# A two-layer hybrid decoder on one core: the last four retention gates as a block product of seven, and a few pieces of work moved

## The chip, the cores and the metric

The kernel runs on one NeuronCore of a Trainium2 chip. It is written so that one program computes the whole decoder. TensorE (PE) multiplies, ScalarE (ACT) and VectorE (DVE) take its results out of PSUM and prepare operands in SBUF, GpSimd (POOL) issues a part of the transfers, and SyncE (SP) the rest. The metric is the time of one execution on the device in microseconds (us); of several runs the median is given. Everything is float32 at the boundary.

## The reference

Two layers on 512 tokens of width 1024. With `x` the stream, one layer is

```
h  = rmsnorm(x) ; z = h @ w_in
aq, ak, av, rq, rk, rv, rg, ga, gb = split(z)
A  = window_attention(rope(aq), rope(ak), av, sinks)          # 8 heads, window 128
B  = retention(rq, rk, rv)                                    # 4 heads, 256 values each
B  = B * rsqrt(mean(B*B per head) + eps) * silu(rg)
y  = sigmoid(ga) * (A @ w_a) + sigmoid(gb) * (B @ w_b)
x  = x + y @ w_out
x  = x + relu(rmsnorm(x) @ w_up)**2 @ w_down
```

and a last rmsnorm follows. The part `rg` is 1024 columns of `z`: eight chunks of 128, two for each retention head. `silu(rg)` gates the retention's normalised output.

## The kernel before, in words

**Products.** A number is held as a sum of two rounded halves, `hi` and `lo`, and each product is three matmuls: hi by hi, hi by lo, lo by hi (`products`, L390 to L392). Activations lie transposed: 128 features on the partitions, 512 tokens (`T`) along the columns, so that `xh[:, k, :]`, `xl[:, k, :]` are the halves of eight feature tiles `k`. The scale 1/rms of the tokens (`rstd`) is applied behind the products.

**Weights.** They come in units of 128x1024. `unit_order` lists them; `unit` hands out the next and has those up to three ahead (`SPLIT`) split: ScalarE rounds `hi` (L338), VectorE subtracts for `lo` (L339). Four buffers each hold `hi` and `lo`, five hold the raw unit. SP's queue loads them in that order.

**A chunk** (`chunk`) is 128 output columns for all tokens: 8 tiles `k` by 3 matmuls of 512 columns, one unit of weights.

**A block product of seven.** The value projection (`values`, for `rv`), the output projection (`output`, for `wo`) and the MLP's blocks are made from seven products of half size where the plain way needs eight. They need sums and differences of quarters of the weights and of the activations. For the weights, POOL's queue writes sums into DRAM with accumulating transfers (`sum_steps`), and VectorE adds two more (`add_values`, L318); the jobs of `sum_steps` are let go one by one by `pace`, which every second call copies one column on POOL and issues the next step behind it. For the activations, `Turned` loads `x` again, four tiles at a time into two buffers (`load`, L878), and makes the differences and their splits (`build`, L888 to L896): `turned[1]` to `turned[4]`. `build(0)` makes the first half of all of them, `build(2)` the second.

**Order.** The program is written in the order in which it should run, and a scheduler then orders the instructions of each engine; the order is fixed when the kernel is built, and each engine takes its instructions one after the other. `issue_after` binds what stands in it to come behind a given instruction. Attention and retention are generators (`background`) that are moved on a step at a time from within the chunks.

**A layer** runs so: queries, keys and values of the attention (`group`, then two chunks); eight chunks of `gate_a`, with the attention in between; `qk(0)`; gate chunks `rg` 0 to 3 (`put_rg`); the attention's end (`drain`), its last output `whole` split into `a_h` and `a_l`; `qk(1)` with `turned.build(0)`; gate chunks `rg` 4 and 5; the A projection (`w_a`, four units, result into `mixed` at L1142) with `turned.build(2)` behind its second unit; `values`; `qk(2)`, `qk(3)` with the retention of heads 0 and 1; gate chunks `rg` 6 and 7; four chunks of `gate_b`; half of the B projection (`w_b`, a `group`); the other four chunks of `gate_b`; the other half of `w_b`; `output`; the MLP.

A gate chunk's result is scaled (L988) and put through `silu` (L997, L998) where it stands. In `Head`, `outputs` copies the retention's output out of PSUM into a tile `rr` (L1044) and squares it for the norm (L1046); `finish` multiplies the gate with the inverse norm (L1066), then with `rr` (L1067), and splits the result into `ret`.

The **MLP** begins with `sum_input(0)` in the first up projection and `sum_input(2)` within the first down block (`down(0, ...)`), each making the differences of the MLP's input and their splits (L525 to L539). In the last layer `turn_x` transposes `x` (L1259) and writes it out for the final sums: the first half within `output`, the second, for four token blocks, in the first up projection. In layer 1 the first `group` multiplies all high halves first (`by_halves`, L405), and the ssq matmuls of `Rms.finish` (L608) spread the factors over the partitions.

Names with `r_` and a number, and `late`, are SBUF tiles of a pool of slots, used for whatever is split.

Of the kernel before, what the change touches and what calls it, by code (L numbers as in the profile page):

```python
# [17 lines left out]
P = 128  # L18
# [25 lines left out]
N_IN = 38  # L44
# [12 lines left out]
def unit_order(layer):  # L57

    order = [("w_in", i) for i in range(4 + 2 + 8 + 2 + 4 + 2 + 2)]
    order += [("w_a", i) for i in range(4)]  # L60
    order += [("rv", part, u) for part in range(7) for u in range(2)]
    order += [("w_in", i) for i in range(24, 34)]
    order += [("w_b", i) for i in range(4)]
    order += [("w_in", i) for i in range(34, 38)]
# [51 lines left out]
def decoder(ctx, tc, xT, x_first, w_in, w_rv, w_a, w_b, w_wo, w_up, w_pair, w_down, w_end, tables, decay, band, g_last, out):  # L116
# [63 lines left out]
    def load_until(n):  # L180
# [27 lines left out]
    MIXING = {"rv": w_rv, "wo": w_wo}  # L208
    sums_mix = {
        name: [dram.tile([2, P, 2 * UNIT], F32, name=f"sums_{name}{l}") for l in range(DEPTH)] for name in MIXING  # L210
    }

    def sum_steps(layer):
# [8 lines left out]
        for name, at in (("rv", 0), ("wo", 14)):  # L222
            jobs[at:at] = [(sums_mix[name][layer][u], MIXING[name][layer, u], 2 * UNIT) for u in range(2)]
# [90 lines left out]
    def add_values(i):  # L314
        part = order[i][2]
        if part in (2, 4):
            raws[i] = raws.pop(i - 2)
            nc.vector.tensor_tensor(raws[i], raws[i], raws.pop(i - 4), ALU.add)  # L318
# [75 lines left out]
    latest, behind = [None], []  # L394

    def by_halves(banks, weights, moving, ks, cols, meanwhile):

        hi, lo = weights
        for w, low in ((hi, 0), (lo, 0), (hi, 1)):
            if meanwhile and w is lo:  # L400
                meanwhile()
            for j, k in enumerate(ks):
                for c, ps in enumerate(banks):
                    first, final = k == 0 and w is hi and not low, k == KD - 1 and low
                    latest[0] = nc.tensor.matmul(ps, w[:, cols(j, c)], moving[k][low], start=first, stop=bool(final)).ins  # L405
# [177 lines left out]
    class Rms:  # L583
# [30 lines left out]
    def layer_body(layer):  # L614
# [366 lines left out]
        def put_rg(i):  # L981
            def put(ps):
# [6 lines left out]
                if i >= 4:  # L989
                    pace(rg[i])  # L990
                    silu(i)

            return put

# [13 lines left out]
        class Head:  # L1008
# [5 lines left out]
            def scores(self, js):  # L1014
# [14 lines left out]
                if js[-1] == NB - 1:  # L1029
                    slots.give(*rq.pop(h), *rk.pop(h))  # L1030
                    self.rr, self.sq = [], []

            def outputs(self, e):
# [7 lines left out]
                if e == 0:  # L1041
                    self.both = big("rr")
                r = self.both[:, e, :]
                nc.scalar.activation(r, ps, AF.Copy)  # L1044
                q = temp("sq")
                nc.scalar.activation(q, ps, AF.Square)  # L1046
                pace(r)
                self.rr.append(r)
# [29 lines left out]
        def retention(pair):  # L1078
# [23 lines left out]
            while 4 * pair + 3 not in rg:  # L1102
                yield
# [23 lines left out]
        for i in (4, 5):  # L1127
            chunk("w_in", layer, xs, put_rg(i))

# [19 lines left out]
        load_decay(0)  # L1149
        values(turned)  # L1150
# [5 lines left out]
        for i in (6, 7):  # L1156
            chunk("w_in", layer, xs, put_rg(i))
# [7 lines left out]
        for c in range(4):  # L1165
# [48 lines left out]
        TOKENS = (slice(0, H), slice(H, T))  # L1214
# [23 lines left out]
        for c in range(4, KD):  # L1238
# [18 lines left out]
        def turn_x(ps, b, i):  # L1257
# [10 lines left out]
            t = gain_tile[:, 2, :] if b == NB - 1 and i else temp("y")  # L1268
# [11 lines left out]
        def output():  # L1280
# [23 lines left out]

            def both(t):
                return t.rearrange("p (a t) -> p a t", t=H)
# [53 lines left out]
            ms.free(3, 4)  # L1360
            put(1, 0, b, -1)
# [30 lines left out]
        def sum_input(ks):  # L1392
# [9 lines left out]
            sums.rest(ks, b, (2, 3))  # L1402
# [328 lines left out]
        def first_hooks():  # L1731
            used = []

            def at0():
                used.append(column_factors())
                sum_input(0)

            def at1():
                if last:
                    used.append(bank(ps_aux, "xt"))  # L1740
                    for n in range(NB):
                        turn_x(used[n % 2], n, 1)

            return at0, at1

        for e in range(N_BLOCK):
# [15 lines left out]
            else:  # L1762
                down(e, into, None if e else lambda: sum_input(2))
# [42 lines left out]
def _w_in_units(w):  # L1806
# [20 lines left out]
    units += _units_chunks(w, O_RG + T + r(2 * P))  # L1827
    units += qk(2) + qk(3)
    units += _units_chunks(w, O_RG + T + 2 * P + r(2 * P))
# [12 lines left out]
def _mixing_blocks(w):  # L1842
# [8 lines left out]
    return blocks  # L1851

# [44 lines left out]
def _laid_out(x, g_mix, w_in, sinks, w_a, w_b, w_out, g_mlp, w_up, w_down, g_final):  # L1897
# [11 lines left out]
        "w_in": _stack(w_in, _w_in_units),  # L1909
        "w_rv": _stack(w_in, lambda w: _mixing_blocks(w[:, O_RV : O_RV + D])),  # L1910
# [30 lines left out]
```

## Time and profile before

| what | us |
|---|---|
| three runs | 1461.82, 1461.87, 1464.63 |
| the profiled execution | 1464.35 |
| its span, first to last instruction | 1462.3 |
| TensorE busy | 1450.0 |
| VectorE busy | 1169.0 |
| ScalarE busy | 969.0 |
| POOL busy | 222.3 |
| mean granted TensorE clock | 0.999 |

The profile's page and views give starts and durations in us from the span's start. "PE" is TensorE's multiplying, "PEld" its loading of weights, which overlaps. A matmul's end is modelled and includes its way through the array, so two that follow each other overlap in the list; how long a row of them takes is read from their starts. In a timeline row the last bracket is the idle time before it and what ended it. The chain of waits is followed back from the last instruction to what released each step.

### The profile page before, as it was taken

Reading aid. Unit: us, or ns where it says so; the run is one execution under the profiler, and the core shown is the slowest. Engines: PE = TensorE matmul, PEld = TensorE weight load, DVE = VectorE, ACT = ScalarE, POOL = GpSimd, SP = SyncE. Lnnn points to the kernel's source line nnn. Section 1 sums busy time; section 2 is a strip of 40 time slices with the busy share of each in tenths; the row PEclk is TensorE's granted clock in tenths of the full one; section 3 lists DMA queues with packets and bytes.
Section 4 is the critical chain, followed back from the end, with each engine's and each line's share of the span. In section 5 each row is a group of like instructions: output and inputs, shape, how many; then the busy total and the mean of one; then the engine's idle time right before and its main releaser. Section 6 shows DMA issues by size and latency. Waiting matters only on the chain.

```text
span 1462.3 us, 22150 instructions
## 1 busy us (share of the span) xinstructions
PE 1450.0 (99%) x8041; PEld 1265.4 (87%) x8041; DVE 1169.0 (80%) x1762; ACT 969.0 (66%) x1592; POOL 222.3 (15%) x329
## 2 busy tenths in 40 slices
PE   9999999999999999999999999999999999999998
PEld 7888888888988999999888888888889799999997
DVE  6978876876898888888778788687778988788885
ACT  6657556543687777777756575565437777777775
POOL 0011012112101111111201110112120111111120
PEclk9999999999999999999999999999999999999999
DMA  7598369899745777666955983797885477777664
GB/s 257 177 288 225 103 174 299 232 244 255 224 119 195 192 197 190 165 184 179 307 178 172 290 222 111 217 291 219 222 210 174 137 198 201 191 192 197 178 185 146
DMA packets 96428, 297.57 MB, mean 203 GB/s; under 512 B 11328, under 2 KB 11456, under 8 KB 90432
## 3 DMA queue, kind: packets, MB, share of 16 engines
q0 software_dynamic: 35936, 125.58, 37.2%
q1 hardware_dynamic: 59664, 169.27, 33.4%
q8 instruction: 63, 1.03, 0.3%
q10 hardware_dynamic: 720, 1.31, 0.2%
q14 instruction: 45, 0.37, 0.1%
HBM read 256.54 MB, written 115.87 MB: 255 GB/s over the span
## 4 chain that ended last, share of the span: by engine, by line
PE 96%; ACT 1%; DMA 1%; DVE 1%; issue 0%; DVEq 0%; ACTq 0%
PE mm L390 23%; PE mm L391 23%; PE mm L392 23%; PE wo L1296 5%; PE b L390 3%; PE b L391 3%; PE b L392 3%; PE rv L392 2%; PE rv L390 2%; PE rv L391 2%; PE mm L405 2%; PE score L773 1%; PE pT L738 1%; PE r L392 1%; PE r L391 1%; PE r L390 1%
## 5 line engine op out<-in xcount | busy, mean ns | idle before, releaser
L338 ACT ACTIVATE hi<-raw 128x1024 fp32r<-128x1024 f32 (+1 forms) x387 | 394.1, 1021 | 263.4 <-PE mm L391 146.9
L339 DVE TENSOR_TENSOR lo<-raw,hi 128x1024 fp32r<-128x1024 f32 (+1 forms) x388 | 452.7, 1174 | 107.4 <-ACT hi L338 105.3
L390 PE MATMUL mm<-xh,hi 128*128 128x512 f32 (+1 forms) x976 | 343.8, 356 | 1.8 <-ACT xh L413 1.0
L391 PE MATMUL mm<-xl,hi 128*128 128x512 f32 (+1 forms) x976 | 344.6, 356 | 0.0
L392 PE MATMUL mm<-xh,lo 128*128 128x512 f32 (+1 forms) x976 | 340.4, 355 | 0.0
L390 PEld LDWEIGHTS mm<-xh,hi 128*128 128x128 f32 x976 | 185.2, 190 | 27.7 <-ACT xh L413 1.7
L391 PEld LDWEIGHTS mm<-xl,hi 128*128 128x128 f32 x976 | 185.3, 190 | 24.2
L392 PEld LDWEIGHTS mm<-xh,lo 128*128 128x128 f32 x976 | 183.9, 190 | 23.6
L391 PE MATMUL mm<-r,hi 128*128 128x256 f32 (+1 forms) x608 | 189.2, 311 | 0.0
L392 PE MATMUL mm<-r,lo 128*128 128x256 f32 (+1 forms) x608 | 189.0, 311 | 0.0
L390 PE MATMUL mm<-r,hi 128*128 128x256 f32 (+1 forms) x608 | 186.6, 311 | 0.5 <-ACT mm L1471 0.5
L390 PEld LDWEIGHTS mm<-r,hi 128*128 128x128 f32 x608 | 115.8, 190 | 8.8 <-ACT mm L1471 0.7
L391 PEld LDWEIGHTS mm<-r,hi 128*128 128x128 f32 x608 | 115.8, 190 | 8.0
L392 PEld LDWEIGHTS mm<-r,lo 128*128 128x128 f32 x608 | 115.8, 190 | 6.3
L1619 POOL DMA_DIRECT2D y<-eu x56 | 62.4, 1354 | 374.4 <-DVE eu L1604 373.8
L391 PE MATMUL mm<-lo,r 128*128 128x512 f32 (+1 forms) x276 | 104.3, 387 | 0.0
L392 PE MATMUL mm<-hi,r 128*128 128x512 f32 (+1 forms) x276 | 101.3, 387 | 0.0
L390 PE MATMUL mm<-hi,r 128*128 128x512 f32 (+1 forms) x276 | 98.4, 390 | 0.9 <-ACT eu L1614 0.6
L390 PE MATMUL b<-hi,r 128*128 128x512 f32 x180 | 70.5, 392 | 1.6 <-DVE eu L1604 1.2
L391 PE MATMUL b<-lo,r 128*128 128x512 f32 x180 | 70.3, 390 | 0.0
L1296 PE MATMUL wo<-r,hi 128*128 128x256 f32 x384 | 69.4, 283 | 0.0
L392 PE MATMUL b<-hi,r 128*128 128x512 f32 x180 | 67.9, 390 | 0.0
(323 smaller groups left out, 2682.5 us busy)
## 6 DMA issues: line engine op xcount, KB each, us to landing
raw<-w_in_in SPq DMA_DIRECT2D x73, 512.0 KB, 5.8
sums_down<-w_down_in POOLq DMA_DIRECT2D x30, 1024.0 KB, 11.6
sums_up<-w_pair_in POOLq DMA_DIRECT2D x56, 512.0 KB, 10.9
raw<-w_down_in SPq DMA_DIRECT2D x45, 512.0 KB, 7.6
raw<-w_pair_in SPq DMA_DIRECT2D x84, 256.0 KB, 3.7
y<-y POOLq DMA_DIRECT2D x63, 256.0 KB, 9.4
y<-eu POOLq DMA_DIRECT2D x61, 256.0 KB, 8.1
raw<-sums_down SPq DMA_DIRECT2D x30, 512.0 KB, 7.4
```

The costliest lines, as they stand in the source:

```text
L338: state["high"] = nc.scalar.activation(hi[:, at], raw[:, at], AF.Copy).ins
L339: nc.vector.tensor_tensor(lo[:, at], raw[:, at], f32(hi[:, at]), ALU.subtract)
L390: nc.tensor.matmul(ps, ah, bh, start=start and i == 0, stop=False, **more)
L391: nc.tensor.matmul(ps, ah, bl, start=False, stop=False, **more)
L392: latest[0] = nc.tensor.matmul(ps, al, bh, start=False, stop=stop and i == n - 1, **more).ins
L405: latest[0] = nc.tensor.matmul(ps, w[:, cols(j, c)], moving[k][low], start=first, stop=bool(final)).ins
L738: nc.tensor.transpose(pt[:, i * P : (i + 1) * P], sm[:, at : at + P], ident)
L773: nc.tensor.matmul(ps[:, g * w : (g + 1) * w], q_s[g][:, c, at], part[:, keys], start=i == 0, stop=i == 1)
L1296: latest[0] = nc.tensor.matmul(o, w[:, cols], v, start=start and first and n % 2 == 0 and w is hi and v is vh, stop=final and w is lo, ski ...
L1619: nc.gpsimd.dma_start(y[:, 2 * j + m, i * T : (i + 1) * T], t, **how)
```

## The change

The last four gate chunks of each layer leave the unit order and become a block product of seven over 512 features, 256 columns and the two halves of the tokens. Its function, `last_gates`, runs between the A projection and `values`:

```diff
-    order = [("w_in", i) for i in range(4 + 2 + 8 + 2 + 4 + 2 + 2)]
+    order = [("w_in", i) for i in range(4 + 2 + 8 + 2 + 4 + 2)]
     order += [("w_a", i) for i in range(4)]
+    order += [("rg", part, 0) for part in range(7)]
     order += [("rv", part, u) for part in range(7) for u in range(2)]
...
-        for name, at in (("rv", 0), ("wo", 14)):
+        for name, at in (("rv", 0), ("rg", 0), ("wo", 15)):
...
+        def last_gates(turned):
+            a, b, c = (bank(ps_mm, "rg") for _ in range(3))
+            two = [big("z") for _ in range(2)]
+            def multiply(ps, moving, start=True):
+                hi, lo = unit("rg", layer)
+                for k, (vh, vl) in enumerate(moving):
+                    for n in range(2):
+                        o, cols = ps[:, n * H : (n + 1) * H], slice((2 * k + n) * P, (2 * k + n + 1) * P)
+                        for w, v in ((hi, vh), (hi, vl), (lo, vh)):
+                            nc.tensor.matmul(
...
+            multiply(a, quarter(0, 0))
+            nc.scalar.activation(b, a, AF.Copy)
+            multiply(c, turned[1])
+            five = keep(c, -1)
+            multiply(b, turned[2], False)
+            sum_two = keep(b, 1)
+            multiply(a, quarter(1, 0), False)
+            put(0, 0, a, 1)
+            multiply(c, quarter(1, 1), False)
+            put(0, 1, c, 1, sum_two)
+            done(0)
+            multiply(b, turned[3], False)
+            put(1, 1, b, -1, five)
+            multiply(b, turned[4], False)
+            put(1, 0, b, -1)
+            done(1)
...
-        for i in (4, 5):
-            chunk("w_in", layer, xs, put_rg(i))
...
         load_decay(0)
+        last_gates(turned)
         values(turned)
...
-        for i in (6, 7):
-            chunk("w_in", layer, xs, put_rg(i))
...
-        for c in range(4):
+        for c in range(6):
             gate_tile(c)
             chunk("w_in", layer, xs, gate(gates[c]))
...
-        for c in range(4, KD):
+        for c in range(6, KD):
             gate_tile(c)
```

`put` scales by `rstd` and `done` applies `silu` to two chunks. The weights of the block are laid out as four quarters on the host (`_gate_block`), and one job of `sum_steps` sums them.

The retention's output is gated where it leaves PSUM, and no copy is kept:

```diff
-                r = self.both[:, e, :]
-                nc.scalar.activation(r, ps, AF.Copy)
                 q = temp("sq")
                 nc.scalar.activation(q, ps, AF.Square)
-                pace(r)
+                z = rg[2 * h + e]
+                nc.vector.tensor_tensor(z, ps, z, ALU.mult)
+                pace(z)
...
                     nc.vector.tensor_tensor(z, z, self.inv, ALU.mult)
-                    nc.vector.tensor_tensor(z, self.rr[e], z, ALU.mult)
+                    pace(z)
```

The three smaller edits: the end of `sum_input` is returned and called behind the first down block; the low products of `by_halves` are bound behind the last ssq matmul that `spread` holds; two of the four second-half transposes go into `output`.

```diff
+                    with tc.issue_after(spread[0]) if low and spread else ExitStack():
...
-                nc.tensor.matmul(ps, ones, part, start=i == 0, stop=i == 1)
+                spread[:] = [nc.tensor.matmul(ps, ones, part, start=i == 0, stop=i == 1).ins]
...
-            sums.rest(ks, b, (2, 3))
+            return lambda: sums.rest(ks, b, (2, 3))
...
-                down(e, into, None if e else lambda: sum_input(2))
+                down(e, into, None if e else lambda: rest.append(sum_input(2)))
+                if e == 0:
+                    rest.pop()()
...
             multiply(b, ms[4], False)
+            if last:
+                for n in (2, 3):
+                    turn_x(bank(ps_aux, "xt"), n, 1)
             put(1, 0, b, -1)
```

**Where instructions come to stand.** Line numbers in the rows are those of the kernel that they are from; the changed kernel's L394 to L396 are L390 to L392 of the one before, L343 is L339, L418 is L411, L1659 is L1604, L929 is L922.

First, TensorE in layer 1, ahead of the A projection (`mm<-r_87`, `mm<-r_81`: the halves `a_h` and `a_l`). Before, these are the last rows ahead of it; 55 matmuls, 7 of `qk(1)` and 48 of `rg` 4 and 5, stand between the attention's last matmul (`pv`) and it:

```order
L390 MATMUL mm<-xh,hi 128x512
L391 MATMUL mm<-xl,hi 128x512
L392 MATMUL mm<-xh,lo 128x512
L390 MATMUL mm<-r_87,hi 128x512
L391 MATMUL mm<-r_81,hi 128x512
```

In the changed kernel, from the last `pv` and the last of the 7 matmuls on (`ret` are scores of the retention, `rv<-xh,ones` clears a bank):

```order
L396 MATMUL mm<-xh,lo 128x512
L929 MATMUL rv<-xh,ones 128x512
L394 MATMUL ret<-late 128x512
L395 MATMUL ret<-late 128x512
L396 MATMUL ret<-late 128x512
L394 MATMUL ret<-late 128x384
L395 MATMUL ret<-late 128x384
L396 MATMUL ret<-late 128x384
L394 MATMUL mm<-r_87,hi 128x512 x4
L395 MATMUL mm<-r_81,hi 128x512
```

The 48 matmuls are gone, seven others moved there, and four that read `a_h` alone stand ahead of the first that reads `a_l`. In layer 0 nine matmuls of `qk(1)` stand there in place of seven, with the same rows behind them.

Second, TensorE at the end of the gates' block in layer 0. Behind the product with `turned[3]`, 24 matmuls of `values` come before the product with `turned[4]` (`r_87`, `r_88`), which goes into the bank that `put(1, 1, b, ...)` reads:

```order
L394 MATMUL rv<-hi,xh 128x512
L395 MATMUL rv<-lo,xh 128x512
L396 MATMUL rv<-hi,xl 128x512
L1015 MATMUL rg<-r_87,hi 128x256 x2
L1015 MATMUL rg<-r_87,lo 128x256
```

These are the last three of the 24 and the first of `turned[4]`; layer 1 has the same.

Third, VectorE in layer 1's first down block, where the evacuations `eu` stand among the splits of the MLP's input (`sums`). Before:

```order
L339 TENSOR_TENSOR lo<-raw,hi 128x1024
L537 SCALAR_TENSOR_TENSOR sums<-sums,xg 128x512
L1604 SCALAR_TENSOR_TENSOR eu<-mm,columns,eu 128x512
L411 TENSOR_TENSOR r_83<-sums,r_83 128x1024
L411 TENSOR_TENSOR r_87<-sums,r_87 128x1024
L1604 SCALAR_TENSOR_TENSOR eu<-b,columns,eu 128x512
```

Now:

```order
L418 TENSOR_TENSOR r_83<-sums,r_83 128x1024
L343 TENSOR_TENSOR lo<-raw,hi 128x1024
L1659 SCALAR_TENSOR_TENSOR eu<-mm,columns,eu 128x512
L418 TENSOR_TENSOR r_87<-sums,r_87 128x1024
L1659 SCALAR_TENSOR_TENSOR eu<-mm,columns,eu 128x512
L1659 SCALAR_TENSOR_TENSOR eu<-b,columns,eu 128x512 x2
```

One split moved ahead of the first `eu`, the other did not move behind the last. Layer 0 had this order already and keeps it.

More of the change, by code (lines that the diff above doesn't have):

```diff
@@ L42 @@
 O_GB = O_GA + D
-N_IN = 38
+N_IN = 34
 N_BLOCK = 8
@@ L314, in add_values @@
     def add_values(i):
-        part = order[i][2]
+        name, part = order[i][1:3]
         if part in (2, 4):
-            raws[i] = raws.pop(i - 2)
-            nc.vector.tensor_tensor(raws[i], raws[i], raws.pop(i - 4), ALU.add)
+            n = TALL[name]
+            raws[i] = raws.pop(i - n)
+            nc.vector.tensor_tensor(raws[i], raws[i], raws.pop(i - 2 * n), ALU.add)
     def split_until(n):
@@ L392, in products @@
             latest[0] = nc.tensor.matmul(ps, al, bh, start=False, stop=stop and i == n - 1, **more).ins
-    latest, behind = [None], []
+    latest, behind, spread = [None], [], []
     def by_halves(banks, weights, moving, ks, cols, meanwhile):
@@ L1740, in at1 @@
                     used.append(bank(ps_aux, "xt"))
-                    for n in range(NB):
-                        turn_x(used[n % 2], n, 1)
+                    for n in range(2):
+                        turn_x(used[n], n, 1)
             return at0, at1
+        rest = []
         for e in range(N_BLOCK):
```

70 lines of the change are left out of this document (47 added, 23 removed).

## The prediction

> **What bounds the kernel now.** I read the page first: its busy times, then its part 4, the chain that ended last.
>
> ```profile
> span 1462.3 us, 22150 instructions
> PE 1450.0 (99%) x8041; PEld 1265.4 (87%) x8041; DVE 1169.0 (80%) x1762; ACT 969.0 (66%) x1592; POOL 222.3 (15%) x329
> PE 96%; ACT 1%; DMA 1%; DVE 1%; issue 0%; DVEq 0%; ACTq 0%
> ```
>
> TensorE is the bound in nearly all of the span: 96% of the chain is its own work. So an edit counts only in two ways, by the time its matmuls take back to back, and by idle time of TensorE that it opens or closes. The view of TensorE's waits, longest first, says how little idle time is left to close (total, times, longest):
>
> ```profile
> PE b L390 <- DVE eu L1604: 1.2, 1, 1.2
> PE mm L390 <- DVE rot L635: 0.6, 1, 0.6
> PE mm L390 <- ACT eu L1614: 0.6, 1, 0.6
> PE b L390 <- ACT r L410: 0.4, 1, 0.4
> ```
>
> Three edits touch the places of these four: 1.2 is the MLP's start in layer 0, 0.4 and 0.6 are the same place in layer 1, 0.6 at `rot` is the spread factors. None is near the retention gates. A matmul's listed duration includes its drain, so the price of one is the distance from start to start. It comes from runs of equal matmuls in the chain:
>
> ```profile
> 16.04 0.91 PE mm L390 x4
> 1090.48 34.40 PE wo L1296 x288
> 1125.75 5.65 PE wo L1296 x48
> 401.03 5.83 PE wo L1296 x48
> ```
>
> 512 columns cost 0.91/4 = 0.227 us, 256 columns (the output projection, already a block product of seven) 34.40/288 = 0.1194 us, a little over half.
>
> **The change part by part.** *Fewer columns.* In each layer four gate chunks go: 4 x 24 = 96 matmuls of 512 columns, 21.8 us. Seven products come: 7 x 24 = 168 matmuls of 256 columns, 168 x 0.1194 = 20.1 us. That is 1.7 less a layer, **-3.4 us** for two. Bounds: the two shorter runs have 0.1177 and 0.1215, by which it would be -4.0 or -2.8. I take the long run, since its operands have the shapes and the order of the new block. [...]
>
> *Vector and scalar work of the block.* It splits seven units where four were split: 3 more splits, 2 adds of 128x1024, a copy and two keeps a layer. Each has the price of a row:
>
> ```profile
> L339 DVE TENSOR_TENSOR lo<-raw,hi 128x1024 fp32r<-128x1024 f32 x354 | 430.4, 1221 | 90.7 <-ACT hi L338 88.6 <-PE wo L1296 0.5
> L318 DVE TENSOR_TENSOR raw<-raw 128x1024 f32<-128x1024 f32 x16 | 19.5, 1220 | 0.2
> L1044 ACT ACTIVATE rr<-r 128x512 f32<-128x512 f32 x16 | 9.6, 598 | 10.1 <-PE r L392 10.1
> L997 ACT ACT_TABLE_LOAD x2 | 2.6, 1283 | 0.0
> ```
>
> I cost them at nothing. One unit per 24 matmuls (2.9 us) is just the ratio of the output projection, which ran 288 matmuls without a wait; uncovered, each split or add would cost 1.2. The product that must wait until VectorE has read its bank (`turned[4]`) stands behind 24 matmuls of the value projection (5.4 us) in the order. The 16 `rr` copies that go (9.6 us) and two more table loads (1.3 each) are ScalarE's, which is 66% busy; VectorE keeps its count, one multiply from PSUM for one from SBUF. Six gate chunks instead of four ahead of the B projection, and two behind it, are the same matmuls in place of rg 6 and 7.
>
> *What stood between the attention and the A projection.* This is the term that I rest on. Gate chunks 4 and 5 (48 matmuls) stood there and are gone. The A projection needs the last split of the attention's output. Layer 1, on TensorE, ScalarE and VectorE (start, duration):
>
> ```profile
> 872.02 0.39 PE L759 MATMUL pv<-r,r 128*128 128x512 f32 x1
> 872.25 0.39 PE L392 MATMUL mm<-xh,lo 128*128 128x512 f32 x1
> 884.72 0.39 PE L390 MATMUL mm<-r,hi 128*128 128x512 f32 x1
> 871.77 1.27 ACT L760 ACTIVATE whole<-pv 64x512 f32<-64x512 f32 x2 [4.15 <-PE pv L759]
> 873.06 1.15 ACT L997 ACTIVATE sig<-z 128x512 f32<-128x512 f32 x2
> 874.24 0.60 ACT L631 ACTIVATE rot<-mm 64x512 f32<-64x512 f32 x1
> 874.85 0.59 ACT L632 ACTIVATE rot<-mm 64x512 f32<-64x512 f32 x1
> 875.47 1.06 ACT L338 ACTIVATE hi<-raw 128x1024 fp32r<-128x1024 f32 x1
> 876.43 0.61 ACT L410 ACTIVATE r<-whole 128x512 fp32r<-128x512 f32 x1
> 876.68 1.22 DVE L339 TENSOR_TENSOR lo<-raw,hi 128x1024 fp32r<-128x1024 f32 x1
> 877.82 0.69 DVE L411 TENSOR_TENSOR r<-whole,r 128x512 fp32r<-128x512 f32 x1
> 259.62 0.33 PE L390 MATMUL ret<-r 128*128 128x384 f32 x1
> 260.15 0.40 PE L390 MATMUL mm<-xh,hi 128*128 128x512 f32 x1
> ```
>
> TensorE leaves the last pv at 872.25 and comes to the A projection at 884.72; the high half is there at 877.04, the low one at 878.51. So 6.2 us are spare now. In the changed order 7 matmuls of qk(1) follow the last pv (1.59), one clearing matmul (0.23) and six score matmuls that were pulled ahead: three of 512 columns (0.68) and three of 384 (260.15 - 259.62 = 0.53). TensorE is through at 872.25 + 3.03 = 875.28. The engines' queues from pv to this split hold the same operations as now, so the halves come when they did. Four matmuls read the high half alone and run at 877.1 (1.8 us idle), to 878.0; the fifth reads the low half, 878.57 (0.6 idle): **+2.4 us**. Layer 0 has nine matmuls of qk(1) there, 0.45 more cover, and the same queue behind its last pv: **+1.9 us**. Behind the waiting matmul stand the whole A projection and the gates' block; ScalarE and VectorE wait for nothing of it. Bounds for both layers: 0, if the split came 2.4 earlier; 5.7, if the first four had to wait for the low half too (0.7 more each). I take the rows as they stand, with the order as built.
>
> *x's turned forms.* `turned.build(2)` must now end before the block's second product instead of 11 us later. Its last x tile is loaded into a buffer that `build(0)` gives back:
>
> ```profile
> 889.42 0.53 POOL L878 DMA_DIRECT2D xg<-spill  x1 [9.80 <-DVE r L411]
> 894.59 0.73 ACT L888 ACTIVATE xg<-xg,x 128x512 f32<-128x512 f32 x1 [1.65 <-DMA xg<-spill]
> xg<-spill POOLq DMA_DIRECT2D x4, 512.0 KB, 9.4
> ```
>
> In the changed order sixteen VectorE rows lie between the split of `whole` and the last use of that buffer, fifteen of 0.69 and one split of 1.22: it is free about 878.5 + 11.6 = 890.1. The tile lands 5.2 later at 895.3, and two scalings of 0.73, seven VectorE rows of 0.69 and one split of 1.22 end the form at 902.8. TensorE ends the A projection at 878.57 + 92 x 0.227 = 899.4, the first product at 902.3, and reads the late forms half a product on, 903.7. Margin 0.9, so nothing; a rival below takes it away.
>
> *MLP input forms.* In layer 0 VectorE's order around the wait is row for row what it was, the deferred split (`r_85<-sums`) still ahead of the evacuation that TensorE waits for. So 1.2 stays. In layer 1 the order becomes layer 0's: 0.4 + 0.6 goes, layer 0's 1.2 comes, less one group of four transposes that stretches TensorE there:
>
> ```profile
> 446.46 0.74 DVE L1604 SCALAR_TENSOR_TENSOR eu<-mm,columns,eu 128x512 f32<-128x512 f32 x1
> 447.91 0.50 PE b L390
> 1153.28 0.50 PE xt L1259 x4
> ```
>
> 1.2 - 0.5 - 1.0 = **-0.3**. The transposes themselves are as many as before, in the MLP's up projection where TensorE waits for none. *Spread factors:* the two ssq matmuls stand at the same distance from the group's end as before; the list `spread` holds layer 0's matmul when layer 1's group reads it. **0**, and 0.6 stays.
>
> *Loads.* Five unit loads of 0.5 MB for four a layer, and one more 1 MB sum on POOL's queue, both issued before the attention's middle: nothing, and a late one would show as a wait of the split.
>
> A matmul behind a wait stands in the chain with 0.50 where its neighbours have 0.23; I take 0.1 of that as lost for good, for each of four new waits **+0.4**. Sum: -3.4 + 2.4 + 1.9 - 0.3 + 0.4 = **+1.0 us**. It is made on the profiled execution, 1462.3 of span in a run of 1464.35; the three runs have the median 1461.87 (1461.82 to 1464.63), 2.5 below that run. Put on the median: **1462.9**.
>
> **The rivals.** *No wait at the A projection* (0.18): the split comes earlier since the queues run ahead. For it: ScalarE idled 4.15 before the pv. Against: that idle time ends with the pv itself. -3.4 - 0.3 = -3.7: 1458.2.
>
> *The turned forms come late* (0.18): slower. Place: the last x tile's DMA. It took 5.2, but the median of the four is 9.4; it decides from 0.9 more. At 9.4 it is 4.2 - 0.9 = 3.3 in layer 1, and in layer 0, whose tiles come from another array with a shorter median, 7.4 - 5.2 - 0.9 = 1.3:
>
> ```profile
> xg<-xT_in POOLq DMA_DIRECT2D x4, 512.0 KB, 7.4
> ```
>
> +4.6: 1467.5. Against: the tile that was loaded alone at this place, the row above, took 5.2.
>
> *The clock drops* (0.05). TensorE began the kernel slow (the last two rows are the stretches from 0 to 8 and from 446 to 452 us: the busy times of PE, PEld, DVE, ACT and POOL, then granted clock, DMA share and GB/s):
>
> ```profile
> 1.07 3.78 PE L370 MATMUL warm<-ones 128*128 128x512 f32 x8 [1.07 <-DVE ones L365]
> 5.84 2.08 PE L390 MATMUL mm<-xh,hi 128*128 128x512 f32 x4 [1.00 <-ACT xh L413]
> 0.00:8.00 8.00, 5.94 (x13) 4.25 (x14) 2.94 (x7) 4.62 (x9) 1.93 (x12) 1.00 0.78 255
> 446.00:452.00 6.00, 4.80 (x26) 3.92 (x26) 6.00 (x8) 3.75 (x6) 2.92 (x6) 1.00 0.87 290
> ```
>
> Some 16 matmuls took about 0.45 instead of 0.227, 3.5 us in all. If two idles of 1.8 and 0.6 within 3.3 us bring that back in both layers: +7, 1469.9. Against: behind the longest wait, 1.2, the granted clock in the last row is 1.00; but the row of the slow start has 1.00 too. [...]
>
> *The MLP move works* (0.07), the order not being what decides: both waits go, 1.2 + 1.0 rather than 0.3: 1461.0.
>
> **How the numbers follow.** Forecast 0.52, with its own range 1461.0 to 1465.0. The median of a few runs tells 0.2%, 2.9 us: faster is below 1458.9, slower above 1464.8. Faster: most of the first rival, 0.14. Slower: the second and third, and the forecast's upper end, 0.30. Within: 0.56. The range 1458.5 to 1468.0 leaves out half of the first rival, the third and the second's end, about 0.2.
>
> **What would show it.** The view of TensorE's waits should name two new ones, a matmul on the A projection's line for the ScalarE split of `whole`, 1.8 and 1.4, and for the VectorE split, about 0.6 each; the block's 168 matmuls should take 20.1; the wait for `eu` should stand in both layers and the one for `rot` stay. It is wrong if the A projection starts without a wait, if a matmul of `rg` waits for a split, or if the retention's outputs wait for a bank.

## The result and the profile after

The changed kernel took 1476.27 us in the median of four runs (1475.43 to 1478.36), the kernel before 1461.88 beside it: a ratio of 1.0089, 95% interval 1.0077 to 1.0102. It is slower by 0.9%, some 13 us by that ratio, where 1462.9 was predicted. (The executions of the kernel before, and of most others here, lie in two groups some 2.4 us apart, on which see the start in the last section; a median therefore moves by up to 2 us with how many fall in each, and below spans of profiled executions stand beside medians.)

The page's busy times and chain by engine, after:

```profile
span 1473.9 us, 22472 instructions
PE 1451.4 (98%) x8185; PEld 1271.8 (86%) x8185; DVE 1181.1 (80%) x1776; ACT 974.5 (66%) x1590; POOL 229.7 (16%) x335
PE 90%; DMA 3%; issue 3%; DVE 2%; ACT 1%; POOL 1%; DVEq 0%; POOLq 0%; ACTq 0%
```

TensorE's busy time rose by 1.4 us, the span by 11.6, and the chain has 3% of DMA where it had 1%, and 90% of TensorE where it had 96%: it leaves TensorE somewhere. The view of TensorE's waits (total, times, longest) names the place:

```profile
PE wo L1351 <- DVE lo L343: 7.0, 1, 7.0
PE mm L394 <- ACT r L417: 3.0, 3, 1.7
PE b L394 <- DVE eu L1659: 1.9, 2, 1.2
PE mm L394 <- DVE rot L642: 0.6, 1, 0.6
PE mm L395 <- DVE r L418: 0.5, 2, 0.3
```

The last row and two of the three times of the second are the waits at the A projection that the prediction rests on (the third time, 0.2, is at the B projection); the third and fourth rows are where it said that they would stay. The first is new and was in no part of it: once, 7.0 us, a matmul of the *output* projection, in layer 0. The chain of waits at that place, in order of time (start, duration, what):

```profile
370.69 10.45 DMA sums_last<-sums_down
381.14 0.35 issue
381.48 0.83 POOL sums_last L245
382.31 1.47 POOL x L1307 x3
383.77 8.62 DMA x<-xT_in
...
392.47 0.09 DVE x L1373
...
393.08 1.23 DVE lo L343
...
394.35 3.78 PE wo L1351 x16
```

Read upwards: the matmul waits for the low half of its weights, whose split stands on VectorE behind an add to `x` (L1373), which waits for the load of layer 0's `x` tiles, which POOL issued at 382 because its queue stood behind the second of two adding transfers into `sums_last`, which waits for the first. Nothing of that is at the gates. In the kernel before, the same queue and the same add (POOL's and VectorE's timelines):

```profile
357.99 0.84 POOL L239 DMA_DIRECT2D sums_last<-w_down_in  x1
365.01 1.14 POOL L1252 DMA_DIRECT2D x<-xT_in  x2 [6.18 <-DVE r L411]
393.75 1.11 POOL L241 DMA_DIRECT2D sums_last<-sums_down  x1
380.26 0.68 DVE L1321 TENSOR_TENSOR x<-x,kept 128x512 f32<-128x512 f32 x1
```

There the `x` loads went out from 365 and the adding transfer 29 us behind the first. After the wait TensorE does not run at once as it did; the stretches 388 to 394 and 394 to 400 us of the changed kernel (busy times of PE, PEld, DVE, ACT, POOL, then granted clock, DMA share, GB/s):

```profile
388.00:394.00 6.00, 0.00 (x0) 0.00 (x0) 1.53 (x2) 0.00 (x0) 0.00 (x0) 0.85 0.68 230
394.00:400.00 6.00, 5.65 (x30) 5.65 (x31) 6.00 (x8) 2.77 (x3) 1.07 (x2) 0.59 0.57 175
```

The clock is 0.59 in the second, and 30 matmuls started in it; 52 did in the six us after. Start to start, 19 of them have 0.213 us for 0.120. From start distances the place costs 7.2 + 0.3 + 19 x 0.093 = 9.2 of the 11.6 us.

### The profile page after: what moved, and what is told of

Read it like the earlier page. It is cut to its first block, busy times and chain, and to the rows that moved or that the text cites. A ratio compares the mean times of both kernels' runs of the same rounds, so it can differ in the third digit from the quotient of the medians.

```text
span 1473.9 us, 22472 instructions
## 1 busy us (share of the span) xinstructions
PE 1451.4 (98%) x8185; PEld 1271.8 (86%) x8185; DVE 1181.1 (80%) x1776; ACT 974.5 (66%) x1590; POOL 229.7 (16%) x335
## 4 chain that ended last, share of the span: by engine, by line
PE 90%; DMA 3%; issue 3%; DVE 2%; ACT 1%; POOL 1%; DVEq 0%; POOLq 0%; ACTq 0%
PE mm L395 21%; PE mm L396 21%; PE mm L394 21%; PE wo L1351 4%; PE rg L1015 3%; PE b L394 3%; PE b L395 3%; PE b L396 3%; PE rv L395 2%; PE rv L394 2%; PE rv L396 2%; PE mm L410 2%; DMA sums_up<-w_pair_in 1%; PE score L780 1%; PE pT L745 1%
## 5 line engine op out<-in xcount | busy, mean ns | idle before, releaser
L342 ACT ACTIVATE hi<-raw 128x1024 fp32r<-128x1024 f32 (+1 forms) x393 | 400.1, 1022 | 255.1 <-PE mm L395 120.0
L343 DVE TENSOR_TENSOR lo<-raw,hi 128x1024 fp32r<-128x1024 f32 (+1 forms) x394 | 458.9, 1174 | 93.7 <-ACT hi L342 90.7
L394 PE MATMUL mm<-xh,hi 128*128 128x512 f32 (+1 forms) x912 | 319.1, 354 | 1.7 <-DVE rot L642 0.6
L395 PE MATMUL mm<-xl,hi 128*128 128x512 f32 (+1 forms) x912 | 319.6, 353 | 0.0
L396 PE MATMUL mm<-xh,lo 128*128 128x512 f32 (+1 forms) x912 | 316.2, 353 | 0.1
L394 PEld LDWEIGHTS mm<-xh,hi 128*128 128x128 f32 x912 | 173.2, 190 | 25.7 <-ACT xh L420 1.3
L395 PEld LDWEIGHTS mm<-xl,hi 128*128 128x128 f32 x912 | 173.3, 190 | 21.9
L396 PEld LDWEIGHTS mm<-xh,lo 128*128 128x128 f32 x912 | 172.2, 190 | 21.5 <-DVE lo L343 0.3
L394 PE MATMUL mm<-r,hi 128*128 128x256 f32 (+1 forms) x608 | 186.2, 312 | 3.4 <-ACT r L417 2.9
L396 PE MATMUL mm<-r,lo 128*128 128x256 f32 (+1 forms) x608 | 189.0, 311 | 0.0
L394 PEld LDWEIGHTS mm<-r,hi 128*128 128x128 f32 x608 | 115.5, 190 | 12.8 <-ACT r L417 4.0
L396 PEld LDWEIGHTS mm<-r,lo 128*128 128x128 f32 x608 | 115.8, 190 | 6.3
L396 PE MATMUL mm<-hi,r 128*128 128x512 f32 (+1 forms) x276 | 100.9, 387 | 0.0
L394 PE MATMUL mm<-hi,r 128*128 128x512 f32 (+1 forms) x276 | 98.3, 389 | 0.3 <-ACT r L417 0.2
L394 PE MATMUL b<-hi,r 128*128 128x512 f32 x180 | 70.6, 392 | 1.9 <-DVE eu L1659 1.9
L283 DVE TENSOR_TENSOR raw<-raw 128x512 f32<-128x512 f32 x56 | 38.5, 687 | 40.5 <-DMA raw<-w_pair_in 32.4
```

The costliest lines, as they stand in the source:

```text
L283: nc.vector.tensor_tensor(raws[i][:, at], last[:, LEFT], last[:, RIGHT], ALU.add)
L342: state["high"] = nc.scalar.activation(hi[:, at], raw[:, at], AF.Copy).ins
L343: nc.vector.tensor_tensor(lo[:, at], raw[:, at], f32(hi[:, at]), ALU.subtract)
L394: nc.tensor.matmul(ps, ah, bh, start=start and i == 0, stop=False, **more)
L395: nc.tensor.matmul(ps, ah, bl, start=False, stop=False, **more)
L396: latest[0] = nc.tensor.matmul(ps, al, bh, start=False, stop=stop and i == n - 1, **more).ins
```

## The experiments

**E1: the sums behind the loads again.** Two more ticks before the last step of layer 0's background sums; every transfer is made.

```diff
             nc.gpsimd.dma_start(sums_last, r11.unsqueeze(1).broadcast_to([P, 2, UNIT]))
             yield
+            yield
+            yield
```

> The changed kernel, with the last step of layer 0's background sums (the two adding transfers into sums_last) issued two ticks later, so that it stands behind the eight x tile loads on POOL's queue and not ahead of them. Every transfer is still made. Queue theory: the x tiles land where they did before the change, the 7.2 us wait at the output projection of layer 0 goes, and with it the slow stretch behind it (some 20 matmuls of 256 columns at 0.21 us for 0.12, 2.2 us in all): 1476.3 - 9.4 = 1466.9. Rival, traffic: the five unit loads for four and the further 1 MB sum keep the transfers late, the wait stays: 1474 or more. Rival, weights: the matmul waited for the low half of its own weights because their load was late; then moving POOL's sums changes nothing: 1476.

1465.15 (11 runs), ratio to before 1.0016 (1.0007 to 1.0024), span 1464.8: 9.1 below the changed kernel. POOL's timeline shows the order that was aimed at:

```profile
365.47 1.15 POOL L1309 DMA_DIRECT2D x<-xT_in  x2 [7.01 <-DVE r L420]
392.32 1.11 POOL L246 DMA_DIRECT2D sums_last<-sums_down  x1
```

On TensorE, VectorE, ScalarE and SP the instructions stand in the very order of the changed kernel; only POOL's order differs. No matmul of the output projection waits any more for a weight split. Traffic and weights are out as causes: both were left as they are. What remains, +2.5 us of span over the kernel before, is what the forecast spoke of.

**E2: the same order in the kernel before.** Nothing of the change; ticks are counted from one, and one more chunk of the B projection counts, so that the sums are issued sooner. (Other steps go out at other times too, and the other engines' order shifts in places.)

```diff
-    pace_count = [0]
+    pace_count = [1]
...
-            quiet[0] = c > 5
+            quiet[0] = c > 6
```

> The kernel before the change, with nothing of the change, but with its ticks counted from one and one more chunk of the B projection allowed to tick, which puts the two adding transfers into sums_last ahead of six of the eight x tile loads on POOL's queue. Queue theory: the copy into sums_last goes at 358 us, the adding transfer takes some 10.5 us and the second waits for it, so the six x loads go at about 379.5 and land 8.2 later, at about 388; VectorE wants the second pair of tiles at 385 and stands 3 to 4 us there; TensorE waits 1.5 to 4: 1463.5 to 1466. Rival, traffic (the changed kernel's additional transfers are what is late): 1461.9, as before.

1468.93 (6 runs), ratio 1.0043 (1.0030 to 1.0057). The chain, in order of time:

```profile
356.60 11.29 DMA sums_last<-w_down_in
...
368.26 10.58 DMA sums_last<-sums_down
...
380.35 7.18 DMA x<-xT_in
...
388.26 1.23 DVE lo L339
...
389.53 2.59 PE wo L1296 x14
```

The mechanism is the same link for link, and TensorE's wait is 3.8 us, at the top of what was expected. The time went beyond it, since the clock fell here too (granted 0.88 from 386 to 392 us and 0.84 from 392 to 398; 15 matmuls at 0.213 for 0.120, 1.4 us) and the shifted ticks made a wait of 1.1 us at another place. So the queue's order makes this wait without any gate.

**E3 and E4: cover for the A projection.** On E1, the block's first product (x's first quarter) goes where the gate chunks had stood; in E4 the third product also goes ahead of the first that needs a turned form. One unit is loaded twice for it in E3, two in E4. This is E3's:

```diff
+    order += [("rg", 0, 0)]
     order += [("w_a", i) for i in range(4)]
-    order += [("rg", part, 0) for part in range(7)]
+    order += [("rg", part, 0) for part in range(1, 7)]
...
+        block = last_gates(turned)
+        next(block)
         aT = [(a_h[:, c, :], a_l[:, c, :]) for c in range(4)]
```

> The first run's kernel, with the block's first product (24 matmuls of 256 columns, 2.9 us, from x's first quarter) moved ahead of the A projection, where the two gate chunks stood before the change; its weight unit is loaded twice, 0.5 MB more a layer. Cover theory: the waits at the A projection (1.4 + 0.4 in layer 0, 1.8 + 0.4 in layer 1, with 0.1 of restart each 4.5 us) go; but the product with x's turned forms then comes 2.5 us sooner, and VectorE's last split of them ends at 913.8 in layer 1 where TensorE would want it at 911.2, 177.6 and 176.8 in layer 0: a wait of up to 2.7 us comes back: 1466.9 - 4.5 + 2.7 = 1465.1. Rival, queue: the split of the attention's output is pushed back by as much as the cover is long: 1466.9.

> The third run's kernel, with the block's third product (from x's second quarter) also taken out of its place and put right behind the A projection, ahead of the first product with a turned form; one more unit is loaded twice. Cover theory: nothing waits at the A projection and the turned forms have 2.9 us again: 1466.9 - 4.5 = 1462.4, and the rest of the block's 3.4 gained columns is eaten by what else the change moved. Rival, loads: 1 MB more of unit loads a layer makes splits of the block late, each one seen as a wait of a matmul of the block: 1464 or more.

Neither cover theory held: 1467.78 (7 runs), ratio 1.0032 (1.0021 to 1.0043), and 1470.92 (5 runs), ratio 1.0046 (1.0034 to 1.0058), beside E1's 1465.15. In E3's timelines the cover is there, and the wait behind it too:

```profile
871.26 1.23 DVE L323 TENSOR_TENSOR raw<-raw 128x1024 f32<-128x1024 f32 x1 [4.77 <-DMA raw<-w_rg_in]
878.42 0.73 PE L399 MATMUL mm<-r,hi 128*128 128x512 f32 x2 [1.64 <-ACT r L422]
```

The six score matmuls that had been pulled ahead no longer are, so the cover behind the last `pv` grows from 3.0 to 4.5 us and not by the 2.9 of the product. (Two of the block's banks come from the scores' pool in E3, E4 and E8; whether that is why was not tried.) And the block's weight units now come into VectorE's queue ahead of the attention's last sum: an add that waits 4.8 us for its load, then a split. Counted from the last `pv`, the attention's high half comes 1.4 us later than in E1. In layer 1 that is E3's rival, the queue: what the cover gained, the split lost. E4's time lies where its rival put it, but no matmul of the block waits there; it has the waits at the A projection, 1.5 and 0.9 in layer 1, and there the clock fell too. The stretch of 881 to 883 us in E4:

```profile
881.00:883.00 2.00, 1.73 (x4) 1.45 (x5) 2.00 (x5) 2.00 (x4) 0.57 (x1) 0.58 0.53 197
```

**E5, E6, E7: the split itself earlier.** On E1, the last two silus and the rotation of qk(1) are queued behind the attention's last split. E6 also puts the block's third product second; E7 also makes the MLP's second input forms at their old call again.

```diff
-            for i in range(4):
+            for i in range(2):
                 silu(i)
...
+        with tc.issue_after(last_split[0]), tc.issue_after(last_split[1]):
+            for i in (2, 3):
+                silu(i)
         qk(1)
...
-            chunk("w_in", layer, xs, put_ret(rq, h), rate)
+                chunk("w_in", layer, xs, late(put) if h == 1 else put, rate)
```

(`late` does the same for the rotation.) E6 and E7:

```diff
-    order += [("rg", part, 0) for part in range(7)]
+    order += [("rg", part, 0) for part in (0, 3, 1, 2, 4, 5, 6)]
...
-                down(e, into, None if e else lambda: rest.append(sum_input(2)))
-                if e == 0:
-                    rest.pop()()
+                down(e, into, None if e else lambda: sum_input(2)())
```

> The first run's kernel (sums behind the x tiles), with the two last silus and the rotation of qk(1) queued behind the attention's last split on ScalarE and VectorE. Cover theory, as put in the prediction (what TensorE waits for at the A projection is queue time of ScalarE and VectorE, sig 1.15, rot 1.2 and z 1.3 us, that stands between the pv and the split): by the first run's rows the last sum of pv ends 1.4 us after the first pv copy, one weight split of 1.06 comes between, so the high half is there 2.9 us after that copy and the low half 4.1; TensorE needs them 3.5 and 4.4 us after it: no wait there in either layer, 1.37 + 0.43 and 1.82 + 0.44 with 0.1 of restart each gone, 4.5 us. The second product then starts up to 2.5 us sooner against x's turned forms and may wait for those: 1465.2 - 4.5 = 1460.7 without that wait, 1463 with it. Rival, the split itself is late (the pv copies): 1464 to 1465.

> The run before, with the block's third product (from x's second quarter) put second, ahead of the first product with a turned form; no further load. If the turned forms were late by up to 2.5 us in the run before, 24 matmuls of 2.9 us cover that: 1460.7. If nothing was late there, no difference to it. Rival, raw tiles: two raw units are held longer, a weight split of the block is late and a matmul of the block waits: slower than the run before.

> The run before, with the MLP's second pair of input forms made at its old place again (all in the callback of the first down block). As put in the prediction, layer 1's order of ScalarE and VectorE at the MLP's start is then again the one before the change: its waits there, 0.44 + 0.88 + 0.15 + 0.17 us in the first run, become 0.6 + 0.72: 0.3 faster, not to be told by the time but by the view of waits. Rival: the waits there are set by where the work before them ends, not by this order: they stay at 0.9.

1462.9, 1462.64 and 1462.31 (11 runs each), ratios 0.9999 (0.9990 to 1.0008), 1.0004 (0.9995 to 1.0012) and 1.0000 (0.9991 to 1.0009): the time of the kernel before; E5's span is 2.3 us below E1's. ScalarE's timeline of E5 in layer 1, and the one matmul of the A projection that still waits:

```profile
871.58 1.27 ACT L769 ACTIVATE whole<-pv 64x512 f32<-64x512 f32 x2 [4.15 <-PE pv L768]
873.62 1.06 ACT L344 ACTIVATE hi<-raw 128x1024 fp32r<-128x1024 f32 x1 [0.77 <-PE mm L397]
874.59 0.61 ACT L419 ACTIVATE r<-whole 128x512 fp32r<-128x512 f32 x1
875.10 1.14 ACT L1072 ACTIVATE sig<-z 128x512 f32<-128x512 f32 x2
876.59 0.50 PE L397 MATMUL mm<-r,hi 128*128 128x512 f32 x1 [0.38 <-DVE r L420]
```

The waits were queue time, as the prediction had it: with `sig` and the rotation behind the split, 1.4 and 1.8 become 0.17 in both layers. The low half still costs 0.55, because the weight split (`hi<-raw`) waited for a buffer and took its place. No wait for a turned form came back, so E6 had nothing to cover. E7 turned out to issue the very order of E6 on every engine: moving the call of the input forms moves no instruction, and its runs are 11 more of E6. The waits at the MLP's start in layer 1 are 0.44 and 0.87 in both.

**E8 and E10: the rest of the wait.** E8 is E6 with the first product ahead of the A projection; E10 is E7 with the weight split queued behind the attention's split too.

```diff
+    order += [("rg", 0, 0)]
     order += [("w_a", i) for i in range(4)]
-    order += [("rg", part, 0) for part in (0, 3, 1, 2, 4, 5, 6)]
+    order += [("rg", part, 0) for part in (3, 1, 2, 4, 5, 6)]
```

```diff
-            hi, lo = unit("w_a", layer)
+            with ExitStack() as queue:
+                for ins in last_split if u == 0 else ():
+                    queue.enter_context(tc.issue_after(ins))
+                hi, lo = unit("w_a", layer)
```

> The run e6 (split first, third product second) with the block's first product moved ahead of the A projection as well, this time without a second load of its unit. In e6 TensorE still waits 0.17 for the high half and 0.55 for the low half in each layer, with restarts some 1.8 us in all; 2.9 us of matmuls there cover both. Cover theory: 1462.6 - 1.8 = 1460.8, if the turned forms, wanted 1.1 us sooner, are there. Rival, order of splits: the block's unit split now stands in ScalarE's and VectorE's queue between the pv and the A projection, as in the runs e3 and e4, and gives the gain back: 1462.6 or more.

> The run e7 with one more thing queued behind the attention's last split: the weight split that stood between it and the last sum of pv on ScalarE and VectorE (1.06 and 1.22 us). In e7 TensorE waited there 0.17 and 0.55 in each layer, with restarts 1.8 us in all. Cover theory: both waits go, nothing else moves, since the third product now stands ahead of the turned forms: 1.8 faster than e7's 1462.3, 1460.5, and faster than the kernel before by some 0.1 to 0.2%. Rival, weights: the fourth unit of the A projection, split later by about 3 us, or the turned forms, wanted 0.9 sooner, are late instead: 1462 or more, and the view of waits names a matmul of the A projection or of the block that waits for lo or r.

1465.24, ratio 1.0015 (1.0006 to 1.0023), and 1463.23, ratio 1.0005 (0.9996 to 1.0014). In both the A projection starts without a wait, in both layers, and another has taken its place; TensorE's waits in E8, and below in E10:

```profile
PE rg L1026 <- DVE r L421: 2.5, 2, 1.3
```

```profile
PE rv L396 <- ACT hi L344: 2.1, 2, 1.0
```

In E8 the first product with a turned form waits for that form's low half, 1.5 us of start distance in each layer: the wait of the prediction's second rival. That the last x tile was its cause, as that rival had it, is not shown: in the changed kernel that tile of layer 1 landed 3.9 us behind its issue, sooner than the 5.2 that the prediction worked with. In E10 the value projection waits for its weights, 1.2 in each. Three things bound this stretch within 2 us of each other: the attention's split, the turned forms, and the splits of the weight units.

**E9: fewer ticks.** The changed kernel without one of its lines. Its sums fall so late that the two additions into `sums_last` come after layer 0's last block has loaded them; that block works with the copies alone.

```diff
                     nc.vector.tensor_tensor(z, z, self.inv, ALU.mult)
-                    pace(z)
```

> The changed kernel with one line less: the second of its two new ticks in the gating of the retention's outputs (the one in the norm's product) does not count. The background sums are otherwise as in the change, the additional 1 MB sum among them. Tick theory: it is the number of ticks that put the sums_last transfers ahead of the x loads; with eight ticks fewer in a layer they fall behind them, and the time is the first run's, 1465.2. Rival, the additional sum (one more job in the queue) moved them: then ticks alone do not bring it back as far, or the sums, later all along, make a weight load of the MLP late: above 1468.

1469.16 (8 runs), ratio 1.0041 (1.0028 to 1.0053). Its POOL queue, and a wait that no other kernel here has:

```profile
365.45 1.15 POOL L1306 DMA_DIRECT2D x<-xT_in  x2 [4.34 <-DVE r L418]
776.67 1.09 POOL L244 DMA_DIRECT2D sums_last<-sums_down  x1
```

```profile
PE score L780 <- DMA r<-qlo: 1.7, 2, 1.0
```

The `x` loads go at 365 and the output projection waits for nothing, with the additional sum still in the queue: the ticks moved the transfers. The time is not E1's all the same. The adding transfers now run in layer 1's attention, the first from 777 and the second from 788, just where TensorE waits at 787 to 794 for transfers of `qlo`, 2.4 us by start distances. That the one holds up the other was not tried.

**E11 and E12: ten warming matmuls.** The kernel before, and E7, each with one number changed.

```diff
-WARM = 8
+WARM = 10
```

> The kernel before with ten warming matmuls at the start for eight. What is asked: the times of every kernel here lie in two groups 2.2 to 2.5 us apart (before: 1461.6 to 1462.9 and 1463.8 to 1465.1). Of the profiled executions, those whose first real matmul started at 5.31 to 5.33 us (0.48 us idle behind the warming ones) ran 9 to 11 slow matmuls in all, those that started at 5.43 to 5.84 (0.59 us idle and more) 17 to 18, 1.5 to 2 us more. Gap theory: the idle time between the warming matmuls and the first real one keeps the clock down; two more of them at 0.43 us end at 5.5 us, close the gap, and all executions fall in the lower group: 1461.8, with a spread of 1 us. Rival, the groups have another cause (loads, the start of the profile): two groups as before, or all 0.2 later.

> The run e7 (sums behind the x tiles, split first, third product second, forms undone) with ten warming matmuls for eight. Gap theory: its runs (1461.7 to 1462.3 and 1463.0 to 1464.5) fall in the lower group as well: 1461.8, the same as the run beside it within 0.1%, and faster than the kernel before by about half of 2.4 us in the mean. Rival: two groups as before.

1462.32 (1461.84 to 1462.91) and 1462.27 (1461.54 to 1463.32), 11 runs each, beside 1463.81 (1461.93 to 1464.78) of the kernel before in 21: E11 has no run of the upper group, and E12 one, 1463.32, that lies between the two. The intervals of the ratios, 0.9985 to 1.0003 and 0.9985 to 1.0002, still reach 1, and against each other the two are equal. So no version here is shown to beat the kernel before.

## Why the prediction was wrong

**The step that failed** is the sentence on loads: "Five unit loads of 0.5 MB for four a layer, and one more 1 MB sum on POOL's queue, both issued before the attention's middle: nothing". It priced the sum that was added and not the ticks that issue all of them. A step of the background sums goes out on every second tick. The change takes ten ticks from a layer (eight of the `rr` copies, two of rg 6 and 7; those of rg 4 and 5 never counted, since `pace` is switched off from `qk(1)` into `values`) and brings sixteen (eight behind each of the two gating products): three steps more, for one more job. In POOL's timeline of layer 0, 27 of 28 steps are out before the `x` loads in the kernel before, and all 29 in the changed one (30 of 31 in E1, 26 of 29 in E9). So the last step, two adding transfers that wait for each other, slid ahead of the `x` loads. It cost 9.2 us, shown by E1, which undoes it, and by E2, which brings the same wait about without the change. Tick count and not the added sum moved it: E9. The prediction had a rule for this, that a late load would show as a wait of a split; it did, but the load was `x`, which the change does not touch, and no rival had that place. What the prediction should have counted is each queue that a step is moved past: POOL's order, old and new, at the `x` loads.

**The A projection** was right, and its size too. Layer 1 in the changed kernel:

```profile
886.88 1.19 PE L394 MATMUL mm<-r,hi 128*128 128x512 f32 x4 [1.65 <-ACT r L417]
888.34 0.50 PE L395 MATMUL mm<-r,hi 128*128 128x512 f32 x1 [0.27 <-DVE r L418]
```

By start distances 1.82 and 0.43, where 1.8 and 0.6 were worked out; layer 0 has 1.37 and 0.43 for 1.4 and 0.6. With the restarts it is 4.5 us for 4.7 predicted, and E5 shows that it was queue time.

**The block** took its price: the chain through one stretch of it (start, duration),

```profile
909.53 10.55 PE rg L1015 x88
```

is 0.1199 a matmul for 0.1194, so 336 of them take 40.3 us where 192 of 512 columns took 43.6: -3.3 for -3.4. The unit splits, the added sums, the copies and the gating from PSUM did hide: no matmul of the block waits in the changed kernel.

**x's turned forms** were in time in the changed kernel, with the A projection late; where E8 took its wait away the forms were late by 1.5. So the margin of 0.9 was small enough to be lost, and it was bound to the other term.

**Input forms and spread factors.** The waits for `eu` in layer 0 and for `rot` stayed, as said. Layer 1's gain of 0.3 did not come: 0.60 and 0.72 became 0.44 and 0.87 us, and E6 and E7, which are one order, show that the place of the forms' call moves nothing. What reordered the start there is open; the moved transposes are left, and were not tried alone.

**Not foreseen, and small:** 0.22 and 0.32 us at the B projection in layer 1, with restarts 0.7 us. The sum as measured, by start distances: -3.3 + 4.5 + 9.2 + 0.7 = 11.1 of the 11.6 us of span; the rest is spread over gaps below 0.13.

**The rivals.** The clock's fall did happen, though behind the wait that nobody had foreseen and not at the A projection; its price there was 19 x 0.093 = 1.8 us, and in E4 some 1.6 each time, not 3.5, which was the extra time of the whole start. That it spared the A projection was nearer than a chance of 0.05 says, as the last section shows. Without the 9.2 the measured sum is 1.9 us where 1.0 was forecast, and E1 is 0.16% above the kernel before (0.07 to 0.24) for 0.07 forecast.

## What to carry to other kernels

Where background transfers are issued by a tick that some other code calls, an edit that adds or drops a tick moves all of them: compare the queue's order as a whole, old and new, and look for every transfer that crosses a load with a reader close behind. Here an adding transfer that waited for another held POOL's queue until the first one had landed, 10.5 us, so its place in the queue counted for more than its bytes. And when filler work is taken from ahead of a wait, look for the cure in the order of the waiting engines: here the moved queue entries won back 2.3 us, and the moved matmuls nothing.

## What the runs showed of the hardware

**The start.** The kernel before, E1, E5 to E8 and E10, all with eight warming matmuls, had two groups of times, and the profiled executions show what differs. The first matmuls of E1, of E8, and of E12 (start, duration, count):

```profile
1.06 3.78 PE L376 MATMUL warm<-ones 128*128 128x512 f32 x8 [1.06 <-DVE ones L371]
5.43 2.07 PE L396 MATMUL mm<-xh,hi 128*128 128x512 f32 x4 [0.59 <-ACT xh L422]
```

```profile
1.07 3.78 PE L377 MATMUL warm<-ones 128*128 128x512 f32 x8 [1.07 <-DVE ones L372]
5.33 1.17 PE L397 MATMUL mm<-xh,hi 128*128 128x512 f32 x4 [0.48 <-ACT xh L423]
```

```profile
1.06 3.87 PE L376 MATMUL warm<-ones 128*128 128x512 f32 x10 [1.06 <-DVE ones L371]
5.78 1.19 PE L396 MATMUL mm<-xh,hi 128*128 128x512 f32 x4 [0.84 <-ACT xh L422]
```

In E1 the first four matmuls behind the warming ones take 2.07 us, in E8 1.17; E1's profiled run, 1466.52, is in its upper group and E8's, 1464.66, in its lower one. An idle piece of 0.59 us behind the warming matmuls went with the one, of 0.48 with the other. But the length of that piece alone does not decide it: behind 0.84 us, E12's first four take 1.19. There matmuls had become faster before the piece: E12's ten warming ones take 3.87 us where E11's ten, which leave no piece at all, take 4.63. With ten of them no run of E11 lies above 1462.91, and one of E12's eleven above 1462.61.

**The clock in the middle.** One idle piece of 7.2 us (changed kernel) or 3.8 us (E2) went with matmuls at about half rate: 19 and 15 of them at 0.213 us for 0.120, with a granted clock of 0.59 from 394 to 400 us in the one and 0.84 from 392 to 398 in the other. In E4, 1.5 and 0.9 us idle with five matmuls between went with a fall too: by stretches of 2 us, the granted clock from 881 to 885 is 0.58 and 0.57, with matmuls at 0.43 us for 0.23, and in layer 0, from 153 to 159, it is 0.82, 0.50 and 0.83. In E3, 1.8 and 0.9 with five between, the longer idle time, did not (1.00 from 877 to 887), nor did 1.8 and 0.4 in the changed kernel (1.00 from 882 to 894). So in these runs neither the length of a wait nor the sum of two decides it alone.

In the changed kernel's trace TensorE stands idle from 387.1 to 394.35 us. The granted clock is 1.00 up to 392.1, 5.0 us into that piece, then 0.50 until 399.0, 4.6 us behind the restart, then 1.00 again. What sets these moments, and why E4's waits went with a fall and E3's did not, no run here shows.
